# First stage of a hybrid SSD/MLP mixer: norm in 16 columns, tables and small loads moved, shift and scale between products, last three rows tile by tile

## The chip, the cores and the metric

The kernel runs on one core of a Trainium2 chip. Its engines work side by side, each with an instruction queue of its own: TensorE (PE, matrix products; the loading of its weights is listed apart as PEld), VectorE (DVE), ScalarE (ACT), GpSimd (POOL) and SyncE (SP), which here only issues loads. An instruction whose input is not ready holds up everything behind it on its engine. Large loads run on 16 DMA engines, in the order in which they are issued on a queue.

The metric is the device time of one execution in microseconds, as a median over several.

## What is computed by the reference

One layer (the depth is 1) of a mixer over 256 latent tokens with 256 context tokens as a prefix, all in float32, width 2048. Cut to what matters:

```python
shift, scale, gate = split(silu(c) @ w_ada + b_ada, 3)             # latent tokens
shift_c, scale_c, _ = split(silu(c_ctx) @ w_ada + b_ada, 3)        # context tokens
hc = rmsnorm(ctx, g_pre) * (1 + scale_c) + shift_c
hx = rmsnorm(x, g_pre) * (1 + scale) + shift
zc, zx = hc @ w_in[:, :XBC_W + DT_W], hx @ w_in
# both: depthwise convolution over tokens + SiLU, dt = softplus(z_dt + dt_bias)
y = bidirectional_ssd(...)          # latent scans start from the context's final states
y_a = rmsnorm((y + d_skip * xh) * silu(z_ssd), g_ssd)
y_b = rmsnorm(u * (w_s @ rmsnorm(v, g_v) + b_s) * silu(z_mlp), g_mlp)
x = x + gate * rmsnorm(concat(y_a, y_b) @ w_out, g_post)
```

The change lies in the first part: norm, shift, scale, h, and the first columns of z. What is computed behind it is as it was.

## The kernel before

**Layout.** Activations are held with channels on the 128 partitions and the 512 tokens (256 of context, then 256 latent) in columns. The 2048 channels are 16 blocks of 128, numbered by kt. A product in nearly full float32 precision is made of three: each operand is split into a rounded part (hi) and the rest (lo), and hi x hi, hi x lo and lo x hi are summed in PSUM (`mm3`, L124 to L126).

**The first stage** runs with PE, DVE and ACT in the order in which the program is written (`manual_schedule`). It has these steps.

- *Norm.* x arrives in four loads of four blocks (`xT`, L228). Each block is squared, even ones by ACT (L246), odd ones by DVE (L244); PE sums the squares over the partitions with a matrix of ones into `pss` (L248), one quarter of the partitions for each kt modulo 4. Warming products (L236) stand between. The sums are copied (L252), summed again and spread over all partitions by a product over 512 columns (L254), and Sqrt (L255) and reciprocal (L256) give the scale `rb`, 512 columns on all partitions.
- *Shift and scale.* `ada_mm` multiplies the conditioning vectors with one loaded tile of `w_ada` (1 MB; `ada`), as products with 32 columns of weights each into one of four quarters of the partitions (L209). There are 32 such tiles. They are grouped in units: a unit of one block kt takes two tiles (64 columns a product), a unit of two blocks takes four (128 columns). `ada_fin` ends a unit: DVE transposes the sums (L216), ACT adds biases and gains into `ha` and `hb` (L218, L220). Before, units 0 and 1 have one block, the others two.
- *h.* `make_h(kt)`: DVE multiplies x by scale and norm (L287), ACT adds the shift and rounds to hi (L290), DVE forms lo (L292).
- *Weights.* `wst` holds, for each kt, 64 columns for dt and seven tiles of 128 columns (`FIRST`). `split_st(kt)`: ACT rounds (L279), DVE forms the rests (L280 for dt, L281 for the tiles).
- *Products.* A row is one kt: psdt (two products of 512 columns, L360 and L361), then tiles 0 to 6 by three products each, tiles 3 and 6 over the latent 256 columns only. Each tile has its own PSUM sums over all 16 rows, so no tile is done before row 15. In rows 1 to 13 tiles of shift and scale for later rows, and in rows 1 to 14 `h` of the next, stand ahead of the row's products; in row 0 they stand between and behind them. In row 15 psdt and tiles 4 and 5 come first (`LAST`), then dt is brought to token order by PE (`dt_tok`, L300, L301) and put through a softplus on DVE and ACT (`dt_softplus`, L304 to L314), then come the other tiles.

**Loads** of this stage are issued by SP: x, the tiles of `w_ada` (six buffers) and `wst` (three). A load waits on SP until its buffer has been used. Three small ones (dt bias, A, D skip) are issued by POOL at the head, among constants that POOL builds.

**Behind it** come 25 more tiles of z (`wxbc`, split by L80 and L81), with convolution (L433, L446), SiLU and the SSD scans placed between their products by a list of due times (`later`, `pump`); there the scheduler orders the engines. A tile's PSUM is free again when its convolution has read it. Then follow the latent part (`wlat`) and the output projection.

## Time and profile before

| | |
|---|---|
| runs (median of 3) | 1017.2 us (1014.84 to 1017.51) |
| the profiled execution | 1015.47 us |
| its span, first to last instruction | 1013.7 us |
| mean granted clock of TensorE | 0.992 |
| first product row begins (L360) | 28.59 us |
| last pair of tiles of shift and scale begins (L209) | 120.45 us |
| first product of the next stage begins | 137.28 us |

Times in the profile's lines count from the first instruction. A line of the timeline gives start, duration, engine, line of the code, operation, output and inputs, how many instructions are merged, and in brackets how long the engine had been idle and what ended that. A matrix product's duration runs beyond the start of the next one, since products are pipelined: what a product costs in a stream is the distance of the starts. A line of the waits gives the wait in total, how often, and the longest.

### The profile page before, as it was taken

To read this page: it belongs to the slowest core of one execution; us is meant where nothing else is said; L and a number is where in the kernel's file an instruction comes from. 1 tells how busy PE (TensorE), PEld (TensorE's weight loads), DVE (VectorE), ACT (ScalarE), POOL (GpSimd) and SP (SyncE) were. 2 spreads that over 40 slices of the span, in tenths; PEclk is the share of its full clock that TensorE was granted. 3 is DMA by queue.
4 is the path that set the end of the run, shared out by engine and by line. 5 is a ranking of instruction groups with operands and counts; after the bars stand their busy time and mean duration, and the time that the engine had idled before them with its cause. 6 is when DMAs were issued, how large, how long until landed. Compare 5 with 4: busy or idle time off the path is not lost.

```text
span 1013.7 us, 14056 instructions
## 1 busy us (share of the span) xinstructions
PE 988.3 (97%) x5628; PEld 802.7 (79%) x5628; DVE 630.5 (62%) x954; ACT 469.1 (46%) x657; POOL 118.9 (12%) x161
## 2 busy tenths in 40 slices
PE   6899999989999999999999999999999999999996
PEld 2788887768887878787888888887888888888885
DVE  4544499886657575666567767666555564445626
ACT  3433357643534353444645433455565563346512
POOL 1000012652322322224000000000000000000000
PEclk9899999999999999999999999999999999999999
DMA  9999642122223222234787777774455545556622
GB/s 353 414 416 416 277 191 83 45 81 83 83 84 110 73 109 83 84 110 147 293 310 266 283 283 289 268 283 169 179 192 178 195 166 208 187 188 245 255 81 83
DMA packets 30033, 198.82 MB, mean 196 GB/s; under 512 B 3552, under 2 KB 3696, under 8 KB 7312
## 3 DMA queue, kind: packets, MB, share of 16 engines
q1 hardware_dynamic: 28224, 192.44, 50.5%
q0 software_dynamic: 1024, 4.28, 1.6%
q10 hardware_dynamic: 720, 1.20, 0.3%
q8 instruction: 44, 0.72, 0.3%
q14 instruction: 21, 0.17, 0.0%
HBM read 195.81 MB, written 2.10 MB: 195 GB/s over the span
## 4 chain that ended last, share of the span: by engine, by line
PE 77%; issue 9%; DVE 5%; DMA 5%; POOL 2%; ACT 1%; SPq 0%; DVEq 0%; POOLq 0%; ACTq 0%
PE psx L124 9%; PE psx L126 9%; PE psx L125 9%; PE pa L862 8%; PE pa L863 8%; PE pa L864 7%; PE pm L907 3%; PE pm L908 3%; PE pm L909 3%; PE psada L209 3%; PE pq L907 2%; PE pq L909 2%; PE pq L908 2%; DVE acc L446 2%; DMA ada<-in_wada_dram 2%
## 5 line engine op out<-in xcount | busy, mean ns | idle before, releaser
L81 DVE TENSOR_TENSOR lo_w<-w,hi_w 128x1024 fp32r<-128x1024 f32 x234 | 288.9, 1240 | 203.5 <-ACT hi_w L80 203.3
L80 ACT CAST hi_w<-w 128x1024 fp32r<-128x1024 f32 x234 | 245.8, 1052 | 314.2 <-PE pa L864 144.2
L862 PE MATMUL pa<-hi_w,hhi 128*128 128x512 f32 x512 | 201.9, 395 | 0.0
L863 PE MATMUL pa<-lo_w,hhi 128*128 128x512 f32 x512 | 199.8, 390 | 0.1
L864 PE MATMUL pa<-hi_w,hlo 128*128 128x512 f32 x512 | 199.4, 389 | 0.0
L124 PE MATMUL psx<-hhi,hi_w 128*128 128x512 f32 (+1 forms) x400 | 152.9, 382 | 2.4 <-DVE acc L446 2.4
L125 PE MATMUL psx<-hlo,hi_w 128*128 128x512 f32 (+1 forms) x400 | 146.3, 366 | 0.0
L126 PE MATMUL psx<-hhi,lo_w 128*128 128x512 f32 (+1 forms) x400 | 146.1, 365 | 0.0
L862 PEld LDWEIGHTS pa<-hi_w,hhi 128*128 128x128 f32 x512 | 96.2, 188 | 20.9 <-issue 1.6
L864 PEld LDWEIGHTS pa<-hi_w,hlo 128*128 128x128 f32 x512 | 96.1, 188 | 20.0
L863 PEld LDWEIGHTS pa<-lo_w,hhi 128*128 128x128 f32 x512 | 96.2, 188 | 19.9 <-DVE lo_w L81 0.5
L124 PEld LDWEIGHTS psx<-hhi,hi_w 128*128 128x128 f32 x400 | 75.6, 189 | 15.7 <-issue 5.0
L125 PEld LDWEIGHTS psx<-hlo,hi_w 128*128 128x128 f32 x400 | 75.6, 189 | 12.8 <-issue 1.9
L126 PEld LDWEIGHTS psx<-hhi,lo_w 128*128 128x128 f32 x400 | 75.5, 189 | 12.5 <-issue 0.2
L446 DVE SCALAR_TENSOR_TENSOR acc<-psx,pc,acc 128x248 f32<-128x248 f32 (+1 forms) x204 | 84.4, 468 | 1.4 <-ACT acc L433 0.7
L723 DVE SCALAR_TENSOR_TENSOR junk<-gate,cb 128x2048 bf16<-128x2048 f32 x16 | 36.6, 2289 | 22.2 <-DMA gate<-in_wada_dram 22.2
L907 PE MATMUL pm<-hi_w,hhi 128*128 128x512 f32 x128 | 50.0, 390 | 0.0
L908 PE MATMUL pm<-lo_w,hhi 128*128 128x512 f32 x128 | 49.9, 390 | 0.0
L909 PE MATMUL pm<-hi_w,hlo 128*128 128x512 f32 x128 | 49.7, 389 | 0.0
L124 PE MATMUL psx<-hhi,hi_st 128*128 128x512 f32 (+1 forms) x112 | 41.2, 368 | 0.0
L125 PE MATMUL psx<-hlo,hi_st 128*128 128x512 f32 (+1 forms) x112 | 40.6, 362 | 0.0
L126 PE MATMUL psx<-hhi,lo_st 128*128 128x512 f32 (+1 forms) x112 | 40.5, 362 | 0.0
(224 smaller groups left out, 1264.0 us busy)
## 6 DMA issues: line engine op xcount, KB each, us to landing
w<-in_wlat_dram SPq DMA_DIRECT2D x64, 1024.0 KB, 4.8
ada<-in_wada_dram SPq DMA_DIRECT2D x32, 1024.0 KB, 14.7
w<-in_wout_dram SPq DMA_DIRECT2D x32, 1024.0 KB, 4.8
w<-in_wxbc_dram SPq DMA_DIRECT2D x25, 1024.0 KB, 4.8
gate<-in_wada_dram SPq DMA_DIRECT2D x16, 1024.0 KB, 5.1
wst<-in_wst_dram SPq DMA_DIRECT2D x16, 480.0 KB, 14.1
xT<-in_xch_dram SPq DMA_DIRECT2D x4, 1024.0 KB, 10.1
xf<-in_xtok_dram SPq DMA_DIRECT2D x2, 1024.0 KB, 5.6
```

The source lines that it names most:

```text
L80: nc.scalar.copy(hi, raw)
L81: nc.vector.tensor_tensor(lo, raw, hi.bitcast(F32), op=ALU.subtract)
L124: nc.tensor.matmul(ps, lhsT=whi, rhs=hhi[k][:, s], start=start, stop=False)
L125: nc.tensor.matmul(ps, lhsT=whi, rhs=hlo[k][:, s], start=False, stop=False)
L126: nc.tensor.matmul(ps, lhsT=wlo, rhs=hhi[k][:, s], start=False, stop=stop)
L446: nc.vector.scalar_tensor_tensor(ao, zi, cw[:, k : k + 1], ao, op0=ALU.mult, op1=ALU.add)
L862: nc.tensor.matmul(pa[tk], lhsT=hhi[k][:, t], rhs=whi[:, w], start=k == 0, stop=False)
L863: nc.tensor.matmul(pa[tk], lhsT=hhi[k][:, t], rhs=wlo[:, w], start=False, stop=False)
L864: nc.tensor.matmul(pa[tk], lhsT=hlo[k][:, t], rhs=whi[:, w], start=False, stop=k == KT - 1)
L907: nc.tensor.matmul(p, lhsT=yh[:, t], rhs=whi[:, w], start=j == 0, stop=False)
L908: nc.tensor.matmul(p, lhsT=yh[:, t], rhs=wlo[:, w], start=False, stop=False)
L909: nc.tensor.matmul(p, lhsT=yl[:, t], rhs=whi[:, w], start=False, stop=hf == 0 and j == 15)
```

## The change

- *Head.* The three small loads move from POOL to SP, after the loads that row 4 issues. `sc` is cleared by DVE. Silu of the conditioning vectors and a first Sqrt come ahead of the squares on ACT. The first six tiles of `w_ada` and three `wst` blocks are issued ahead, `wst` 0 right after the first tile.
- *Norm.* The 512 sums are transposed in blocks of 32 (DVE), so that one product with a selecting matrix (`sel`) gives them in 16 columns; Sqrt and reciprocal work on 16 columns; a copy and a second block transpose spread the result over 512 columns again. Two more warming products stand behind the first two tiles of shift and scale.
- *Start.* Split 0 is made ahead of shift, scale and h of row 0.
- *Units.* Four units of one block, then six of two; the layout of `w_ada` in memory follows.
- *Between products.* `row_steps` puts each tile of shift and scale after the first, second or a later product tile of a row, no longer ahead of the row. In rows 0 to 2 `ada_fin`, `make_h` and `split_st` of the next row hang on the second of them; from row 3 on the splits stand at the row's beginning. Row 3 has four tiles, row 12 the last four, then h and split of rows 14 and 15.
- *Last rows.* Rows 13 to 15 run tile by tile: psdt, 4 and 5 of row 13; then psdt, tile 4, tile 5 in rows 14 and 15, dt's turn; then tiles 0, 1, 2, 3, 6 each over all three rows. Split 15 takes a buffer of the ring of `w_ada` tiles.

```diff
-    nc.gpsimd.dma_start(dtc, dtp[0:1].partition_broadcast(P))
...
-    nc.gpsimd.dma_start(dsk, dskip.partition_broadcast(P))
...
-    nc.gpsimd.dma_start(A, dtp[1:2].partition_broadcast(P))
...
     sc = stp.tile([P, KT, 32], F32, name="sc")
-    nc.gpsimd.memset(sc, 0.0)
+    nc.vector.memset(sc, 0.0)
...
-    nc.scalar.activation(sc[:, :, 0:2], sc2, AF.Silu)
-    tc.keep_in_program_order(nc.scalar.activation(sc2[:, 0, 0:1], epsc, AF.Sqrt))
+
+    sel = stp.tile([P, 4, 32], F32, name="sel")
+    nc.vector.tensor_reduce(sel[:, 0], ident.rearrange("p (g m) -> p m g", g=4), axis=mybir.AxisListType.X, op=ALU.add)
+    nc.vector.tensor_copy(sel[:, 1:4], bc(sel[:, 0], 1, 3))
...
-    UNITS = [(0,), (1,)] + [(m, m + 1) for m in range(2, KT, 2)]
+    UNITS = [(m,) for m in range(4)] + [(m, m + 1) for m in range(4, KT, 2)]
 
     def ada_place(ci):
 
-        if ci < 4:
+        if ci < 8:
             return ci // 2, 64, 8 * (ci % 2), 8
-        return ci // 4 + 1, 128, 4 * (ci % 4), 4
-
-    def ada_load(c0):
-        for ci in (c0, c0 + 1):
+        return ci // 4 + 2, 128, 4 * (ci % 4), 4
+
+    def ada_load(ci):
+        if ci < 2 * KT:
             ada_raw[ci] = load_raw(wada[ci], f"ada_{ci}")
...
+    wraw = {}
+
+    def wst_load(kt):
+        w = st3.tile([P, WST], F32, tag="wst", name=f"wst{kt}")
+        nc.sync.dma_start(w, wst[kt])
+        wraw[kt] = w
+
     for t in range(4):
         nc.sync.dma_start(xT[:, 4 * t : 4 * t + 4, :].rearrange("p k t -> p (k t)"), xch[t])
     ada_load(0)
+    wst_load(0)
+    ada_load(1)
+    ada_load(2)
+    ada_load(3)
+    wst_load(1)
+    ada_load(4)
+    ada_load(5)
+    wst_load(2)
+
+    nc.scalar.activation(sc[:, :, 0:2], sc2, AF.Silu)
+    nc.scalar.activation(sc2[:, 0, 0:1], epsc, AF.Sqrt)
 
 
     psw = spt([P, 512], "psw")
...
         nc.tensor.matmul(pss[32 * g : 32 * g + 32, :], lhsT=ones[:, 0:32], rhs=sq, start=k < 4, stop=k >= KT - 4)
         if g == 3:
             warm(1)
+
+
     rb, ss4 = yseg(4), yseg(5)
-    nc.vector.tensor_copy(ss4, pss)
-    psb = spt([P, TOK], "psb")
-    nc.tensor.matmul(psb, lhsT=ones, rhs=ss4, start=True, stop=True)
-    nc.scalar.activation(rb, psb, AF.Sqrt, bias=epsc, scale=1.0 / (32 * D))
-    nc.vector.reciprocal(rb, rb)
+    nc.vector.transpose(ss4, pss)
+    psb = spt([P, KT], "psb")
+    nc.tensor.matmul(psb, lhsT=sel.rearrange("p g m -> p (g m)"), rhs=ss4.rearrange("p (b i) -> p b i", i=32)[:, :, 0],
+                     start=True, stop=True)
+    rc = stp.tile([P, KT], F32, name="rc")
+    nc.scalar.activation(rc, psb, AF.Sqrt, bias=epsc, scale=1.0 / D)
+    nc.vector.reciprocal(rc, rc)
+    nc.vector.tensor_copy(ss4.rearrange("p (b i) -> p b i", i=32), bc(rc, 2, 32))
+    nc.vector.transpose(rb, ss4)
     ada_mm(0)
     ada_mm(1)
+    warm(2)
     psdt = spt([P, TOK], "psdt")
     psx = []
...
     def split_st(kt):
         raw = wraw[kt]
-        hi = wp["spl"].tile([P, WST + 64], F32R, tag="hi", name=f"hi_st{kt}")
-        lo = wp["spl"].tile([P, WST - 64], F32R, tag="lo", name=f"lo_st{kt}")
+        if kt < KT - 1:
+            hi = wp["spl"].tile([P, WST + 64], F32R, tag="hi", name=f"hi_st{kt}")
+            lo = wp["spl"].tile([P, WST - 64], F32R, tag="lo", name=f"lo_st{kt}")
+        else:
+            hl = wp["raw"].tile([P, 2048], F32R, tag="raw", name=f"hl_st{kt}")
+            hi, lo = hl[:, 0 : WST + 64], hl[:, WST + 64 : 2 * WST]
         nc.scalar.copy(hi[:, 64:], raw)
         nc.vector.tensor_tensor(hi[:, 0:64], raw[:, 0:64], hi[:, 64:P].bitcast(F32), op=ALU.subtract)
         nc.vector.tensor_tensor(lo, raw[:, 64:], hi[:, P:].bitcast(F32), op=ALU.subtract)
@@ -314,54 +335,80 @@
         nc.vector.scalar_tensor_tensor(pl, pl, 2.0, s1, op0=ALU.add, op1=ALU.mult)
 
     sp0 = {}
-    wst_load(0)
-    ada_load(2)
-    wst_load(1)
-    ada_load(4)
-    ada_fin(0)
-    make_h(0)
-    sp0[0] = split_st(0)
-    for kt in range(KT):
-        if kt + 2 < KT:
-            wst_load(kt + 2)
-        if kt + 3 < KT:
+
+    def prod(i, kt):
+        whi, wlo = sp0[kt]
+        if i < 0:
+            nc.tensor.matmul(psdt, lhsT=whi[:, 0:P], rhs=hhi[kt], start=kt == 0, stop=False)
+            nc.tensor.matmul(psdt, lhsT=whi[:, 0:P], rhs=hlo[kt], start=False, stop=kt == KT - 1)
+        else:
+            mm3(psx[i], whi[:, (i + 1) * P : (i + 2) * P], wlo[:, i * P : (i + 1) * P], kt,
+                kt == 0 and i < 6, kt == KT - 1 and i != 3, ORDER[FIRST[i]] >= 24)
+
+    ALL = [("m", i) for i in range(-1, NST)]
+
+    def row_steps(kt):
+
+
+        st_ = {n: [] for n in range(1, NST + 1)}
+        if kt < 3:
+            st_[2] = [("a", 2 * kt + 2)]
+            st_[3] = [("a", 2 * kt + 3), ("f", kt + 1), ("h", kt + 1), ("s", kt + 1)]
+        elif kt == 3:
+            st_[1] = [("s", 4)]
+            st_[2], st_[3], st_[4] = [("a", 8), ("a", 9)], [("a", 10)], [("a", 11), ("f", 4), ("h", 4)]
+        elif kt % 2 == 0:
+            st_[1] = [("h", kt + 1), ("s", kt + 1)]
+            st_[2], st_[3] = [("a", 2 * kt + 4)], [("a", 2 * kt + 5)]
+            if kt == FULL - 1:
+                st_[5] = [("a", 30)]
+                st_[6] = [("a", 31), ("f", 9), ("h", 14), ("s", 14), ("h", 15), ("s", 15)]
+        else:
+            st_[1] = [("s", kt + 1)]
+            st_[2], st_[3] = [("a", 2 * kt + 4)], [("a", 2 * kt + 5), ("f", kt // 2 + 3), ("h", kt + 1)]
+        out_ = [("m", -1, kt)]
+        for n in range(1, NST + 1):
+            out_ += st_[n] + [("m", n - 1, kt)]
+        return out_
+
+
+    FULL = KT - 3
+    steps = [("s", 0), ("f", 0), ("h", 0)]
+    for kt in range(FULL):
+        steps += [("l", kt)] + row_steps(kt)
+    steps += [("m", i, FULL) for i in LAST[:3]]
+    for n, i in enumerate(LAST):
+        steps += [("m", i, kt) for kt in range(FULL + (n < 3), KT)]
+        if i in (4, 5):
+            steps.append(("z", i - 4))
+        if n == 2:
+            steps.append(("t",))
+    for what, *ij in steps:
+        if what == "m":
+            prod(*ij)
+        elif what == "a":
+            ada_mm(*ij)
+        elif what == "f":
+            ada_fin(*ij)
+        elif what == "h":
+            make_h(*ij)
+        elif what == "s":
+            sp0[ij[0]] = split_st(*ij)
+        elif what == "l":
+            kt = ij[0]
             ada_load(2 * kt + 6)
-        whi, wlo = sp0[kt]
-        if kt + 1 < KT:
-            sp0[kt + 1] = split_st(kt + 1)
-        steps = [("m", -1)] + [("m", i) for i in range(NST)]
-        if kt == KT - 1:
-            steps = [("m", i) for i in LAST]
-            steps.insert(3, ("t", 0))
-            for i in range(2):
-                steps.insert(steps.index(("m", 4 + i)) + 1, ("z", i))
-        if kt == 0:
-            steps[1:1] = [("a", 2)]
-            steps[3:3] = [("a", 3)]
-            steps[5:5] = [("f", 1), ("h", 1)]
-            steps += [("a", 4), ("a", 5)]
-        elif kt + 1 < KT:
-            a = [("a", 2 * kt + 4), ("a", 2 * kt + 5)] if kt + 2 < KT else []
-            f = [("f", (kt + 1) // 2 + 1)] if kt % 2 else []
-            steps = a + f + [("h", kt + 1)] + steps
-        for what, i in steps:
-            if what == "a":
-                ada_mm(i)
-            elif what == "f":
-                ada_fin(i)
-            elif what == "h":
-                make_h(i)
-            elif what == "z":
-                nc.vector.tensor_copy((z4, z5)[i], psx[4 + i])
-            elif what == "t":
-                dt_tok()
-                dt_softplus()
-            elif i < 0:
-                nc.tensor.matmul(psdt, lhsT=whi[:, 0:P], rhs=hhi[kt], start=kt == 0, stop=False)
-                nc.tensor.matmul(psdt, lhsT=whi[:, 0:P], rhs=hlo[kt], start=False, stop=kt == KT - 1)
-            else:
-                mm3(psx[i], whi[:, (i + 1) * P : (i + 2) * P], wlo[:, i * P : (i + 1) * P], kt,
-                    kt == 0 and i < 6, kt == KT - 1 and i != 3, ORDER[FIRST[i]] >= 24)
+            ada_load(2 * kt + 7)
+            if kt + 3 < KT:
+                wst_load(kt + 3)
+            if kt == 4:
+                nc.sync.dma_start(dtc, dtp[0:1].partition_broadcast(P))
+                nc.sync.dma_start(A, dtp[1:2].partition_broadcast(P))
+                nc.sync.dma_start(dsk, dskip.partition_broadcast(P))
+        elif what == "z":
+            nc.vector.tensor_copy((z4, z5)[ij[0]], psx[4 + ij[0]])
+        elif what == "t":
+            dt_tok()
+            dt_softplus()
...
-    for kt in range(2):
+    for kt in range(4):
         wada[2 * kt : 2 * kt + 2] = ss[:, :, :, kt].reshape(2, 8, P, 256).transpose(0, 2, 1, 3).reshape(2, P, D)
-    for m in range(2, KT, 2):
+    for m in range(4, KT, 2):
```

More of the change, by code (lines that the diff above doesn't have):

```diff
@@ L265, in tile_hybrid_ssd_mlp @@
     psx[3] = psx[3][:, 0:256]
-    wraw = {}
-    def wst_load(kt):
-        w = st3.tile([P, WST], F32, tag="wst", name=f"wst{kt}")
-        nc.sync.dma_start(w, wst[kt])
-        wraw[kt] = w
     def split_st(kt):
         raw = wraw[kt]
-        hi = wp["spl"].tile([P, WST + 64], F32R, tag="hi", name=f"hi_st{kt}")
-        lo = wp["spl"].tile([P, WST - 64], F32R, tag="lo", name=f"lo_st{kt}")
+        if kt < KT - 1:
[4 more added lines that the diff above has]
+            hi, lo = hl[:, 0 : WST + 64], hl[:, WST + 64 : 2 * WST]
         nc.scalar.copy(hi[:, 64:], raw)
```

## The prediction

> **What bounds the kernel now.** The page first, then the time by stretches, then what TensorE (PE) waited for up to 240 us.
>
> ```profile
> span 1013.7 us, 14056 instructions
> PE 988.3 (97%) x5628; PEld 802.7 (79%) x5628; DVE 630.5 (62%) x954; ACT 469.1 (46%) x657; POOL 118.9 (12%) x161
> ```
>
> ```profile
> 40.00:60.00 20.00, 19.92 (x254) 16.39 (x248) 9.98 (x22) 7.50 (x17) 0.00 (x0) 1.00 1.02 416
> ...
> 140.00:160.00 20.00, 19.60 (x99) 16.00 (x98) 19.30 (x40) 10.70 (x14) 0.82 (x3) 1.00 0.16 54
> ...
> 200.00:220.00 20.00, 17.50 (x92) 13.77 (x91) 16.90 (x32) 9.62 (x14) 13.01 (x16) 1.00 0.29 105
> ```
>
> ```profile
> PE psdt L360 <- DVE hi_st L280: 5.4, 1, 5.4
> PE pss L248 <- ACT y L246: 4.6, 2, 3.7
> PE psx L124 <- DVE acc L446: 2.4, 1, 2.4
> ...
> PE psy L641 <- DVE M L624: 0.3, 1, 0.3
> PE psd L497 <- DVE y L480: 0.3, 1, 0.3
> ```
>
> The columns of a stretch are its length, then busy time of PE, weight load, DVE, ACT, POOL, then granted clock, DMA share, GB/s. PE is the bound almost everywhere. In the first stage the loads run at the full 416 GB/s too, yet PE never stands for them after 42 us. There is little to win: the 5.4 us before the first product row, the slow clock behind it, and 3.0 us (2.4 + 0.3 + 0.3) of waits for VectorE (DVE) after the stage, which DVE, full at 140 to 160 us, causes.
>
> **The start.** Before:
>
> ```profile
> 11.99 1.28 ACT L176 ACT_TABLE_LOAD   x1
> ...
> 13.53 1.28 ACT L177 ACT_TABLE_LOAD   x1
> ...
> 14.94 2.42 ACT L246 ACTIVATE y<-xT 128x512 f32<-128x512 f32 x4
> ...
> 19.37 0.69 DVE L252 COPY y<-pss 128x512 f32<-128x512 f32 x1 [1.40 <-PE pss L248]
> ...
> 21.17 1.99 PE L209 MATMUL psada<-ada,sc 128*32 128x64 f32 x128
> 21.28 0.69 ACT L255 ACTIVATE y<-psb,epsc 128x512 f32<-128x512 f32 x1 [3.92 <-PE psb L254]
> 22.00 3.35 DVE L256 RECIPROCAL y<-y 128x512 f32<-128x512 f32 x1 [1.94 <-ACT y L255]
> ...
> 25.27 0.19 DVE L216 STREAM_TRANSPOSE adat<-psada 128x64 f32<-128x64 f32 x1
> ...
> 26.49 0.91 ACT L290 ACTIVATE hhi<-xT,hb 128x256 fp32r<-128x256 f32 x2 [0.42 <-DVE xT L287]
> ...
> 28.59 0.80 PE L360 MATMUL psdt<-hhi,hi_st 128*128 128x512 f32 x1 [5.42 <-DVE hi_st L280]
> ```
>
> Both table loads and their two small activations stand between squares, so four squares run back to back after them. With the tables loaded while ACT waits for x anyway, the squares follow the loads of x:
>
> ```profile
> DMA to landing us min/median/max: 6.7/10.1/13.0
> ```
>
> The fourth load of x, issued at 2.7 us, lands by 15.7. Two squares by each engine (about 0.65 each) end at 17.1 and the last sum at 17.6, against 19.2: 1.5 earlier, so DVE can start at 17.85. The old way from the sums to the scale takes 19.37 to 25.35, 5.98. The new one: a 32-block transpose of 512 columns, a product with 16 columns, Sqrt and reciprocal of 16 columns, a copy of 512, a transpose of 512. No row has such a transpose. The 64- and 128-column ones (0.19 here, 0.32 below) give 2 ns a column and, as an estimate, 1.1 us for 512; bounds are 0.69 (the copy of the same shape) and 3.35 (the slowest row of that shape). I take 1.1, by slope. With 0.7 for the copy, 0.8 for the three small steps and five hand-overs of 0.1 that makes 4.2. The scale is ready at 22.05. The first split, now ahead, costs DVE 1.15; transpose to the end of hhi takes 25.27 to 27.40 = 2.13. First product at 25.4. The small loads that leave the head of the run are worth something too:
>
> ```profile
> q0 software_dynamic: 96, 0.08, 1.3%
> ```
>
> That is 1.3% of 140 us: 1.8 us of all engines. I take 1.0 of it (bounds 0 and 1.8). So 24.4 instead of 28.59: **-4.2** (bounds: +0.3 with both transposes at 3.35, -5.8 with 0.69 and 1.8). The second tile of shift and scale now queues behind the first split's weights. Its load has landed by 22.2 today (the second half of the row at 21.17); 0.49 MB ahead of it cost 1.2 at 416 GB/s, the 1.0 comes off, 1.0 of product and 2.2 of preparation follow: 25.6 at the latest, which I leave to the bounds.
>
> Then the clock:
>
> ```profile
> 22.00:24.00 2.00, 1.17 (x84) 1.00 (x72) 2.00 (x1) 0.00 (x0) 0.00 (x0) 1.00 1.02 426
> 24.00:26.00 2.00, 0.00 (x0) 0.00 (x0) 1.54 (x3) 0.51 (x2) 0.00 (x0) 0.92 1.00 410
> ...
> 30.00:32.00 2.00, 2.00 (x65) 1.83 (x58) 1.23 (x2) 0.09 (x1) 0.00 (x0) 0.50 0.99 413
> 32.00:34.00 2.00, 2.00 (x68) 1.45 (x67) 0.00 (x0) 0.00 (x0) 0.00 (x0) 0.88 1.07 428
> ```
>
> PE stopped at 23.2, the clock fell to half near 25.7 (0.92 is 1.68 us full, 0.32 half) and came back near 32.5. With two warming products and a first row at 24.4, PE stands too briefly for that. What this row lost comes from these:
>
> ```profile
> 41.54 0.50 PE L360 MATMUL psdt<-hhi,hi_st 128*128 128x512 f32 x1
> ```
>
> ```profile
> 113.72 1.96 PE L209 MATMUL psada<-ada,sc 128*32 128x128 f32 x64
> ...
> 120.45 1.95 PE L209 MATMUL psada<-ada,sc 128*32 128x128 f32 x64
> 122.33 0.50 PE L360 MATMUL psdt<-hhi,hi_st 128*128 128x512 f32 x1
> ...
> 127.09 0.39 PE L360 MATMUL psdt<-hhi,hi_st 128*128 128x512 f32 x1
> ...
> 131.75 0.39 PE L360 MATMUL psdt<-hhi,hi_st 128*128 128x512 f32 x1
> ...
> 137.28 0.40 PE L124 MATMUL psx<-hhi,hi_w 128*128 128x512 f32 x1
> ```
>
> A row of products takes 131.75 - 127.09 = 4.66: 0.47 for psdt, 0.70 for a full tile, 0.35 for a latent one. A pair of tiles of shift and scale takes 122.33 - 120.45 = 1.88, 0.94 each (a 64-column one 1.99/2 = 1.0). Row 0 lasted 28.59 to 41.54 = 12.95 and should have taken 4.66 + 2.0 + 3.76 + three switches: 11.0. **-1.95** (upper bound 0, if the clock is slow anyway).
>
> **Between products.** A row with one pair lasts 120.45 - 113.72 = 6.73; less 4.66 and 1.88 leaves 0.19 for switching to the 32-column products and back. Before, they stood in 15 places: two in row 0, the run over its end, one in each of rows 2 to 13. Now there are 29: two a row, three in row 3, four in row 12. 14 x 0.19 = **+2.7** (bounds 0, if the 0.19 belongs to the rows, and 3.5, at 0.25). Units 2 and 3 in 64 columns add 4 x 0.06 = **+0.2**.
>
> In rows 0 to 2 the next row's shift, scale, h and split now all hang on a tile placed after the third product. The chain behind such a tile:
>
> ```profile
> 122.47 0.32 DVE L216 STREAM_TRANSPOSE adat<-psada 128x128 f32<-128x128 f32 x1 [5.52 <-PE psada L209]
> 123.24 0.88 DVE L287 SCALAR_TENSOR_TENSOR xT<-xT,ha,y 128x256 f32<-128x256 f32 x2 [0.46 <-ACT ha L218]
> ...
> 125.66 0.23 DVE L280 TENSOR_TENSOR hi_st<-wst,hi_st 128x64 fp32r<-128x64 f32 x1 [0.41 <-ACT hi_st L279]
> 125.80 1.08 DVE L281 TENSOR_TENSOR lo_st<-wst,hi_st 128x896 fp32r<-128x896 f32 x1
> 126.80 0.87 DVE L287 SCALAR_TENSOR_TENSOR xT<-xT,ha,y 128x256 f32<-128x256 f32 x2
> ```
>
> From the tile's end (122.33) to the split's first part (125.89) are 3.56, for a single unit 3.5. PE has three full and two latent tiles left, 2.8, and 0.1 to switch: 0.6 short, three times, **+1.8** (bounds 0 and 2.9). From row 3 on the split goes ahead and the chain is about a us shorter: covered by those 2.9.
>
> **The last rows.** Row 12 carries four tiles. Behind the last stand transpose, h14, split14, h15, split15 on DVE and ACT, and the order on PE asks for psdt of rows 14 and 15 after only 3.0 us (two tiles, then three products of row 13, 2.92, and 0.1). Split14 comes at 3.56: 0.55 of waiting. Split15: h15 begins 126.80 - 122.33 = 4.47 behind, and h to split takes 125.89 - 123.24 = 2.65: 7.12, while PE is through with row 14's psdt at 4.0. Another 3.1. **+3.6** (bounds 2.6, and 4.9 if a split of the next weights, L81, slips in with its 1.2 to 1.3 a piece). Everything on PE queues behind these two products; nothing else there may pass them.
>
> The clock: the 2.4 us wait near 206 left it at 1.00, the idle time from 23.2 felled it after 2.5. Here 4.1 us pass with 0.47 of work; I take it that it falls. One slow stretch of 2 to 4 us at half speed costs 1 to 2: **+1.5** (bounds 0 and 1.95, what row 0 lost). [...]
>
> PE leaves the stage at 137.28 - 4.2 - 1.95 + 2.7 + 0.2 + 1.8 + 3.6 + 1.5 = 140.9: later by 3.6. In exchange psdt is complete some 13 us ahead of that (the twelve products of tiles 4 and 5 in rows 14 and 15 and all of the other five tiles are still to come, 12 us with dt's turn, and the slow clock), and DVE works on what it did late before:
>
> ```profile
> 135.45 0.41 DVE L301 TENSOR_TENSOR y<-pstok,dtc 128x256 f32<-128x256 f32 x1
> ...
> 150.43 0.41 DVE L480 SCALAR_TENSOR_TENSOR y<-dtt,y 128x256 f32<-128x256 f32 x1
> ```
>
> This chain ended 13 us behind PE's leaving. It starts when tiles 4 and 5 are through, at about 132.5, 8 us before PE leaves instead of 2, and the first convolutions follow tile by tile. That is 6 us and more of head start against waits of 3.0: **-3.0** (bounds 0 and -3.0; nothing else waits there).
>
> **At nothing.** Small loads in row 4: three issues on SP and 1.8 us of DMA; the loads move a row (2.59 MB at 416 GB/s) in 6.2 us against 6.9 for PE, six tiles ahead of use, and make that up in three rows. Without that lead the next tile of shift and scale is late by up to 1.8. The fifteenth row's split holds a load slot until the stage ends, so two later weight loads can queue on SP until 141; the first product that needs them is two tiles (22 us) off. The Silu and Sqrt ahead of the squares wait for a small load and end near 5, while ACT stood until 7.9 for x.
>
> **Sum:** +3.6 - 3.0 = +0.6. The profiled execution took 1015.47 (span 1013.7 and 1.8 around it) and becomes 1016.1; it lies 1.7 below the median of 1017.2, so on the median's scale **1017.8**, its own range 1015 to 1020.
>
> **Rivals**, on the same scale; about 0.3% (3.05 us) is what this kernel's measurement can tell from no change.
>
> 1. The clock holds in the last rows. For it: the clock that held over the 2.4 us near 206; against it: the fall near 25.7. 1017.8 - 1.5 = 1016.3. [...]
> 2. Slower: the waits after the stage stay. Place: the first product tiles after it, up to 206 us, where DVE is full. If DVE spends its head start waiting for PE's late dt products and for weights to split, instead of on dt and convolutions, the 3.0 stay: 1020.8. It decides if the dt addition (L301) starts less than 4.2 us ahead of PE's leaving the stage: the 1.8 of today and the 2.4 that are to be made up.
> 3. The switches cost nothing: 1017.8 - 2.7 = 1015.1. For it: one pair was only seen whole. Against: the products behind a pair take 127.09 - 122.33 = 4.76, the next row's, without one, 4.66.
> 4. The last rows do not wait: -3.6 - 1.5, 1012.7. It needs ACT and DVE to prepare two rows in 3 us; the rows above show 7.1.
> 5. The norm is not sooner, because the wide transposes cost like the reciprocal: 1017.8 + 4.2 = 1022.0.
>
> **Chances.** Forecast 0.36 (0.28 within 0.3%, 0.08 slower); clock holds 0.18 (0.15 within, 0.03 faster); waits stay 0.20 (0.15 slower, 0.05 within); switches free 0.14 (0.08 within, 0.06 faster); last rows do not wait 0.07 (faster); norm not sooner 0.05 (0.04 slower, 0.01 within). Together: faster 0.16, same 0.57, slower 0.27. The range reaches from just above rival 4 to rival 5: 1013.0 to 1022.0.
>
> **What would show it.** The first psdt product near 24.4 at a clock of 1.00; 0.6 us of PE waiting for L280's successor in each of rows 0 to 2; rows 4 to 11 at 6.9 us; a wait of about 3 us for the fifteenth split near 125 and a clock below 1.00 behind it; the first w product near 141; no wait for DVE acc near 206. The forecast is wrong if rows 4 to 11 keep 6.73, if psdt's fifteenth product comes without a wait, or if DVE is still behind at 200 us.

## The result, and the profile after

The changed kernel takes **1031.45 us** (1030.43 to 1032.23 in four runs) against 1016.6 for the kernel of before run beside it: 1.0148 times as long, 95% interval 1.0132 to 1.0163. The forecast was 1017.8 and no change; the time lies outside its range. The page, the waits of PE up to 240 us and the three stretches that were shown of before:

```profile
span 1028.7 us, 14324 instructions
PE 1000.1 (97%) x5760; PEld 805.0 (78%) x5760; DVE 627.9 (61%) x960; ACT 467.9 (45%) x656; POOL 119.6 (12%) x157
```

```profile
PE psd L544 <- DVE y L527: 5.0, 1, 5.0
PE psada L208 <- issue: 3.2, 2, 2.7
PE psdt L342 <- DVE hl_st L301: 2.8, 1, 2.8
...
PE psdt L342 <- DVE hi_st L301: 1.1, 3, 0.5
```

```profile
40.00:60.00 20.00, 16.79 (x295) 12.61 (x294) 5.11 (x12) 4.00 (x9) 0.00 (x0) 0.91 1.02 422
140.00:160.00 20.00, 15.02 (x69) 12.96 (x69) 18.44 (x37) 10.42 (x13) 3.07 (x3) 0.83 0.11 38
200.00:220.00 20.00, 20.00 (x114) 16.18 (x113) 13.96 (x30) 11.33 (x17) 13.21 (x17) 1.00 0.15 54
```

The wait of 5.4 ahead of the first row is gone, and so is that of 2.4 near 206. In their place PE stands in two stretches in which it was full: 3.2 of 20 us at 40 to 60, 5.0 at 140 to 160, with a clock of 0.91 and 0.83 there. The rows behind it, PE's own and in the second fence those of ACT and DVE after the last tile:

```profile
19.68 1.10 PE L208 MATMUL psada<-ada,sc 128*32 128x64 f32 x64 [1.39 <-DMA ada<-in_wada_dram]
...
23.09 0.50 PE L342 MATMUL psdt<-hhi,hi_st 128*128 128x512 f32 x1 [0.40 <-ACT hhi L311]
...
31.23 0.50 PE L342 MATMUL psdt<-hhi,hi_st 128*128 128x512 f32 x1 [0.48 <-DVE hi_st L301]
...
42.52 0.98 PE L208 MATMUL psada<-ada,sc 128*32 128x64 f32 x54
46.15 0.63 PE L208 MATMUL psada<-ada,sc 128*32 128x64 f32 x10 [2.65 <-issue]
...
56.56 0.38 PE L208 MATMUL psada<-ada,sc 128*32 128x128 f32 x2 [0.56 <-issue]
...
61.23 0.49 PE L342 MATMUL psdt<-hhi,hi_st 128*128 128x512 f32 x1
...
118.11 0.39 PE L342 MATMUL psdt<-hhi,hi_st 128*128 128x512 f32 x1
...
127.59 0.39 PE L342 MATMUL psdt<-hhi,hi_st 128*128 128x512 f32 x1
...
130.04 0.50 PE L342 MATMUL psdt<-hhi,hi_st 128*128 128x512 f32 x1 [0.43 <-DVE hi_st L301]
...
133.58 0.50 PE L342 MATMUL psdt<-hhi,hl_st 128*128 128x512 f32 x1 [2.80 <-DVE hl_st L301]
...
152.88 0.71 PE L544 MATMUL psd<-y,tri_lt 128*128 128x96 f32 x2 [4.98 <-DVE y L527]
...
155.00 0.77 PE L122 MATMUL psx<-hhi,hi_w 128*128 128x512 f32 x1
```

```profile
147.94 0.37 ACT L718 COPY y<-psx 128x256 f32<-128x256 f32 x1 [3.41 <-PE psx L124]
148.32 1.28 ACT L496 ACT_TABLE_LOAD   x1
149.62 0.63 ACT L496 ACTIVATE xbc<-acc 128x512 f32<-128x512 f32 x1
150.16 1.98 ACT L80 CAST hi_w<-w 128x1024 fp32r<-128x1024 f32 x2
```

```profile
139.52 0.42 DVE L322 TENSOR_TENSOR y<-pstok,dtc 128x256 f32<-128x256 f32 x1
...
152.32 0.41 DVE L527 SCALAR_TENSOR_TENSOR y<-dtt,y 128x256 f32<-128x256 f32 x1
152.66 1.63 DVE L493 SCALAR_TENSOR_TENSOR acc<-psx,pc,acc 128x252 f32<-128x252 f32 x4
154.21 2.34 DVE L81 TENSOR_TENSOR lo_w<-w,hi_w 128x1024 fp32r<-128x1024 f32 x2
```

The last tile ends at 147.9 (152.88 less 4.98). Two things stand between it and the first w product (a product with the next stage's weights, `hi_w` and `lo_w`). PE comes to the products that end dt (L544) first and waits 4.98 us for their input; they and that wait last until 155.0. In the trace of before the same products (L497) begin at 150.89, 13.6 us behind the first w product, and wait 0.28. And only at 150.16 does ACT begin to split the next weights, behind the copy of the last tile, a table load and a Silu. Of before, the row that answers to it stands during row 14, nine us ahead of the stage's end:

```profile
128.19 3.89 ACT L80 CAST hi_w<-w 128x1024 fp32r<-128x1024 f32 x4
```

With these rows the two spans can be set against each other, stretch by stretch:

| stretch | before | after | difference | forecast |
|---|---|---|---|---|
| start to the first psdt product | 28.59 | 23.09 | -5.5 | -4.2 |
| from there to psdt of row 13 | 93.74 | 104.50 | +10.8 | +2.75 |
| to the end of the last tile | 14.95 | 20.3 | +5.4 | +5.1 |
| to the first w product | 0 | 7.1 | +7.1 | 0 |
| to the end of the span | 876.4 | 873.7 | -2.7 | -3.0 |

The differences add up to 15.1, the spans differ by 15.0. Three rows came out near the forecast, the last of them by another cause (below); two did not, and the experiments are on these. In the runs with this start the first row came at 23.1 to 23.4, in three of them at 24.2 to 24.5; that much is the run's own.

### The profile page after: what moved, and what is told of

It reads as the page before. It is cut to its first block, busy times and chain, and to the rows that moved or that the text cites. A ratio compares the mean times of both kernels' runs of the same rounds, so it can differ in the third digit from the quotient of the medians.

```text
span 1028.7 us, 14324 instructions
## 1 busy us (share of the span) xinstructions
PE 1000.1 (97%) x5760; PEld 805.0 (78%) x5760; DVE 627.9 (61%) x960; ACT 467.9 (45%) x656; POOL 119.6 (12%) x157
## 4 chain that ended last, share of the span: by engine, by line
PE 92%; DVE 3%; ACT 2%; DMA 1%; POOL 1%; issue 1%; SPq 0%; DVEq 0%; ACTq 0%; POOLq 0%
PE pa L909 11%; PE pa L910 11%; PE pa L911 11%; PE psx L122 10%; PE psx L124 9%; PE psx L123 9%; PE psada L208 3%; PE pm L954 3%; PE pm L955 3%; PE pm L956 3%; PE pq L954 2%; PE pq L956 2%; PE pq L955 2%; DMA ada<-in_wada_dram 1%; PE pso L673 1%; PE psy L688 1%
## 5 line engine op out<-in xcount | busy, mean ns | idle before, releaser
L208 PE MATMUL psada<-ada,sc 128*32 128x128 f32 (+1 forms) x1280 | 35.4, 254 | 4.6 <-issue 3.2
L208 PEld LDWEIGHTS psada<-ada,sc 128*32 128x32 f32 x1280 | 27.4, 110 | 15.3 <-issue 12.9
## 6 DMA issues: line engine op xcount, KB each, us to landing
w<-in_wlat_dram SPq DMA_DIRECT2D x64, 1024.0 KB, 4.9
ada<-in_wada_dram SPq DMA_DIRECT2D x32, 1024.0 KB, 10.2
w<-in_wout_dram SPq DMA_DIRECT2D x32, 1024.0 KB, 4.8
w<-in_wxbc_dram SPq DMA_DIRECT2D x25, 1024.0 KB, 4.8
gate<-in_wada_dram SPq DMA_DIRECT2D x16, 1024.0 KB, 5.3
xT<-in_xch_dram SPq DMA_DIRECT2D x4, 1024.0 KB, 7.9
xf<-in_xtok_dram SPq DMA_DIRECT2D x2, 1024.0 KB, 5.6
```

Of the source, the lines that this page charges most:

```text
L208: nc.tensor.matmul(ps[32 * g : 32 * g + 32, 0:n], lhsT=sc[:, k, :], rhs=raw[:, o : o + n], start=k == 0, stop=k == KT - 1)
```

## Experiments

**What holds the next weights back.** Two theories for the 7.1 us: the order in which ACT and DVE were given their work, or the space of the split's buffers, which the fifteenth row's split shares. The first run forces the order:

```
+    split_to(2)
+    early = [getattr(x, "ins", x) for x in last]
     split_to(3)
+
+    def behind(fn, *a):
+        with tc.issue_after(early[0]), tc.issue_after(early[1]):
+            fn(*a)
...
-    nc.scalar.copy(z7, psx[6])
+    behind(nc.scalar.copy, z7, psx[6])
```

(the end of dt and the first two convolutions go through `behind` too; `last` holds the two instructions of the latest split.)

> The changed kernel with one order forced: the first two halves of the next weights (L80, L81) are split ahead of the first convolution, the copy of the last tile and the end of dt on ScalarE and VectorE; the rows are as they were. Changed kernel 1031.5 us. Theory A (the 7.3 us after the stage come from the order of ScalarE and VectorE, where the split stood behind the last tile's copy): the first w product follows the last tile within 1.5 us instead of 7.3, the clock holds there (1.7 more), so 1031.5 - 5.8 - 1.7 = 1024 us (1022 to 1026). Theory B (the space of the split's buffers comes free only with the last row's products): the split waits all the same, 1031.5 within 2. Theory C (the gain is given back, since the convolutions begin later and VectorE is late again near 200 us): up to 3.0 of it is lost, 1027.

1026.82 us, ratio 1.0099 (1.0084 to 1.0114). The rows of PE in the last rows, behind the stage, and later:

```profile
134.24 0.51 PE L343 MATMUL psdt<-hhi,hl_st 128*128 128x512 f32 x1 [2.81 <-DVE hl_st L302]
...
146.85 0.40 PE L123 MATMUL psx<-hhi,hi_w 128*128 128x512 f32 x1
147.08 0.40 PE L124 MATMUL psx<-hlo,hi_w 128*128 128x512 f32 x1
147.74 0.50 PE L125 MATMUL psx<-hhi,lo_w 128*128 128x512 f32 x1 [0.26 <-DVE lo_w L82]
...
217.61 0.47 PE L123 MATMUL psx<-hhi,hi_w 128*128 128x512 f32 x1 [1.97 <-DVE acc L494]
```

The first w product comes 8.15 us sooner, directly behind the last tile, with 0.26 of waiting and a product time of 0.40 instead of 0.77 (at a clock of 0.50 from 152 to 158 us in the changed kernel): theory A, as to the wait. Part of the 8.15 is another thing: behind the same wait of 2.8 in the last rows the products kept 0.39 in this execution (0.63 in the changed kernel), so that the rows took 1.7 us less. From the first w product to the end are 1024.0 - 146.85 = 877.1 instead of 873.7, and 2.0 us of it are a wait for DVE's convolutions again (L494, at 217.6): theory C, as to the total. The edit puts the split ahead and the end of dt behind it, both at once; how the 7.1 divides between the two is not shown. The other theory:

```
+            skip = wp["raw"].tile([P, 2048], F32R, tag="raw", name="skip")
+            nc.vector.memset(skip[:, 0:1].bitcast(F32), 0.0)
             hl = wp["raw"].tile([P, 2048], F32R, tag="raw", name=f"hl_st{kt}")
```

> The changed kernel with the fifteenth row's split in another load slot, whose place the first three split buffers of the next weights do not share; the orders of the engines stay. Theory A (order): no change, 1031.5 us within 2; the first w product stays some 7 us behind the last tile. Theory B (space): the split of the next weights no longer waits for the last row's products, 1031.5 - 7.3 - 1.7 = 1022.5.

1031.27 us, ratio 1.0148 (1.0130 to 1.0167), the same as the changed kernel: the space that the fifteenth split takes is not it. Then the last three rows as a whole, row by row again:

```
-    FULL = KT - 3
+    FULL = KT - 1
...
-    steps += [("m", i, FULL) for i in LAST[:3]]
     for n, i in enumerate(LAST):
-        steps += [("m", i, kt) for kt in range(FULL + (n < 3), KT)]
+        steps += [("m", i, FULL)]
```

(with tiles 30 and 31 in row 13 and the fifteenth split in its own buffer)

> The changed kernel with its last three rows row by row again (tile by tile only in row 15, shift and scale of tiles 30 and 31 in row 13, the fifteenth split in its own buffer); start and insertions stay. Theory A (the tile-by-tile order costs 5.2 in the rows and 7.3 + 1.7 behind them, and brings 2.7 later): 1031.5 - 14.2 + 2.7 = 1020 us (1017 to 1022), and rows 0 to 12 still 10 us longer than before. Rival (the loss is made in rows 0 to 12 and only surfaces behind the stage): 1028 or more.

1019.01 us, ratio 1.0026 (1.0015 to 1.0038). So 12.4 of the 14.8 us that were lost hang on the tile-by-tile order: its own waits and slow clock, and the orders of the engines behind it. Without it the first w product stands at 142.98, directly behind the last tile.

**What takes the start back.** The other loss, +10.8 in rows 0 to 12, remains in that run: from the first row to psdt of row 14, ahead of which both kernels have all tiles of shift and scale, it is +9.8. The start by itself, on the kernel of before:

```
-    nc.vector.tensor_copy(ss4, pss)
+    nc.vector.transpose(ss4, pss)
...
+    sp0[0] = split_st(0)
     ada_fin(0)
     make_h(0)
-    sp0[0] = split_st(0)
     for kt in range(KT):
```

(the whole new norm, the early tables, the late small loads and the order of the first loads; units, rows and last rows are those of before)

> The kernel of before with the new start alone (norm by 16 columns, tables early, small loads in row 4, first split ahead); shift and scale stay at the head of the rows, the last rows row by row. Before: 1016.6 us. Theory A (the start is won and nothing takes it back): first product row at 23.1 instead of 28.6 and no slow clock in row 0, 1016.6 - 5.5 - 1.95 = 1009 us (1008 to 1012). Theory B (the first rows are short of loads or of instructions behind full DMA queues as soon as PE starts sooner): PE waits 2 to 5 us in the rows up to 60 us and it ends at 1012 to 1016.

1015.74 us, ratio 0.9994 (0.9984 to 1.0003): theory B. The first row is at 23.11, and then:

```profile
30.71 2.29 PE L208 MATMUL psada<-ada,sc 128*32 128x128 f32 x64
35.50 1.93 PE L208 MATMUL psada<-ada,sc 128*32 128x128 f32 x32 [2.50 <-DMA ada<-in_wada_dram]
38.05 1.94 PE L208 MATMUL psada<-ada,sc 128*32 128x128 f32 x32 [0.62 <-DMA ada<-in_wada_dram]
39.92 0.80 PE L374 MATMUL psdt<-hhi,hi_st 128*128 128x512 f32 x1
```

Tiles 6 and 7 are asked for at 33 and land at 35.4 and 38.0; the clock falls meanwhile (0.50 at 36 to 40 us, 0.75 at 40 to 44, a psdt product of 0.80). In the kernel of before PE came late enough not to wait for these loads (its waits up to 240 us name none). The changed kernel gets past these loads with units of 64 columns, which need two tiles a row instead of four. It pays in another coin: the two waits inside a tile that the profile puts down to "issue", time in which the engine waited for nothing that the profile shows. Inside a tile a product needs nothing that the tile's first product did not need. Three runs are on these waits and one on the price of the insertions. First, eight instructions fewer ahead of the wait (the run has 5756 products instead of 5760, and as many weight loads):

```
     ada_mm(1)
-    warm(2)
```

> The changed kernel without the two warming products behind the second tile of shift and scale: four product pieces and four weight loads, 8 instructions, fewer on TensorE ahead of the row-2 wait of 2.65 us that no semaphore explains. Theory I (TensorE runs out of instructions at the border of a block of 256): the same wait comes 8 instructions later in the work, behind piece 58 of the 64 of that tile instead of piece 54, about as long. Theory II (the wait belongs to the tile, its load, or a point in time): still behind piece 54, or at 43.5 us wherever that falls. The time is not what is asked; the clock may fall in row 0 and cost up to 2 us.

```profile
44.24 1.08 PE L208 MATMUL psada<-ada,sc 128*32 128x64 f32 x58
47.88 0.31 PE L208 MATMUL psada<-ada,sc 128*32 128x64 f32 x6 [2.56 <-issue]
```

Behind piece 58, as theory I has it (one run, 1032.0 us; a piece is one product of a tile). Then fewer loads queued ahead:

```
-    wp["raw"] = st.enter_context(mkpool(name="raw0", bufs=6, side="right"))
+    wp["raw"] = st.enter_context(mkpool(name="raw0", bufs=4, side="right"))
```

> The changed kernel with four load slots for the tiles of shift and scale instead of six, so that fewer loads are queued ahead. Theory I with the loads as its cause (the block of instructions stands behind loads already queued): the median from issue to landing of those tiles falls from 14.3 us to about 10 and the wait inside a tile near 44 us falls below 1.5 us; TensorE may wait for loads instead, which is a wait at the head of a tile and named as one. Rival (a block takes its 7 us whatever is queued): still 2.65. Time 1028 to 1035.

```profile
45.69 0.41 PE L208 MATMUL psada<-ada,sc 128*32 128x64 f32 x10 [2.12 <-issue]
```

```profile
ada<-in_wada_dram SPq DMA_DIRECT2D x19, 1024.0 KB, 10.2
```

1029.0 us, one run. The loads' median from issue to landing, up to 70 us, falls from 14.3 to 10.2 as expected, the wait only from 2.65 to 2.12: nearer to the rival. The clock holds here (1.00 at 46 to 50, against 0.54 and 0.61). Then the same tiles asked for faster, side by side in rows 0 to 3 and with four slots too, in the kernel with the rows of before from row 4 (below):

```
-            st_[2] = [("a", 2 * kt + 2)]
-            st_[3] = [("a", 2 * kt + 3), ("f", kt + 1), ("h", kt + 1), ("s", kt + 1)]
+            st_[2] = [("a", 2 * kt + 2), ("a", 2 * kt + 3), ("f", kt + 1), ("h", kt + 1), ("s", kt + 1)]
```

> The run with the rows of before from row 4 on (1017.8 us), with four load slots and with the tiles of shift and scale of rows 0 to 3 side by side behind the first product tile: three switches and the waits for the next row's split are gone there, so TensorE asks for the same instructions in less time. Theory I (a block of 256 instructions takes about 7 us to come while the loads run): what the rows win, the waits inside tiles take back; waits that no semaphore explains add up to more than 3 us and row 3 begins at 49 us or later (49.5 with four slots alone). If instructions are no limit: rows of 7.0 us, row 3 at 44.5 to 46.

```profile
37.89 0.28 PE L123 MATMUL psx<-hlo,hi_st 128*128 128x256 f32 x1 [0.43 <-issue]
38.12 0.39 PE L338 MATMUL psdt<-hhi,hi_st 128*128 128x512 f32 x1
39.37 1.92 PE L208 MATMUL psada<-ada,sc 128*32 128x64 f32 x121
44.47 0.32 PE L208 MATMUL psada<-ada,sc 128*32 128x64 f32 x7 [3.19 <-issue]
...
49.86 0.39 PE L338 MATMUL psdt<-hhi,hi_st 128*128 128x512 f32 x1
```

1018.06 us in one run. Theory I: row 3 at 49.86 in spite of shorter rows (some of it is the slow clock behind the wait, 0.70 at 44 to 48 us). And the places can be counted. From the product at 37.89 to piece 121 there are 2 products of the last tile, 2 of psdt, 3 of the first tile and 121, together 128, each with its weight load: 256 instructions. The changed kernel has such a small gap too, 0.3 ahead of the second row here (the other products of this size follow each other in 0.12):

```profile
38.16 0.28 PE L122 MATMUL psx<-hhi,hi_st 128*128 128x256 f32 x1
38.58 0.28 PE L123 MATMUL psx<-hlo,hi_st 128*128 128x256 f32 x1
```

From 38.58 to piece 54 there are again 2 + 2 + 3 + 64 + 3 + 54 = 128. To the third gap, the 0.56 at 56.56, 127 are recorded.

The traces have one more thing on this. The profile's DMA view has a queue of kind instruction, q8, whose packets by their number are PE's (last section). In the changed kernel one begins at 36.2, one at 43.8 and one at 54.2 us, each lasting 0.9 to 1.0, and PE goes on at 38.58, 46.15 and 56.56: 2.3 to 2.4 behind the start of a packet, three times. Together with the wait that moved by four pieces when four products were left out ahead of it, this speaks for the instructions as what PE stands for.

Last, the price of the insertions:

```
-            st_[2], st_[3] = [("a", 2 * kt + 4)], [("a", 2 * kt + 5)]
+            st_[3] = [("a", 2 * kt + 4), ("a", 2 * kt + 5)]
```

(and the same in the odd rows)

> The changed kernel with the two tiles of shift and scale of rows 4 to 12 side by side behind the second product tile instead of one product tile apart: one insertion a row instead of two. If an insertion costs what the rows say (7.11 - 4.66 - 1.88 = 0.57 for two), rows 4 to 11 fall to 6.8 us and the kernel to 1031.5 - 9 x 0.28 = 1029. If the 0.57 belongs to something else in the row (waits for splits, the load of the chip), they stay at 7.1.

```profile
102.32 0.39 PE L342 MATMUL psdt<-hhi,hi_st 128*128 128x512 f32 x1
109.06 0.39 PE L342 MATMUL psdt<-hhi,hi_st 128*128 128x512 f32 x1
```

6.74 a row, against 7.06 for such a row in the changed kernel (the mean over its rows 4 to 11 is (118.11 - 61.23) / 8 = 7.11): a second insertion in a row costs 0.3, a first one the 0.2 that it cost at the row's head. 1027.5 us, one run, in which the products also kept 0.39 behind the last rows' wait of 2.80.

**Put together.** First the new start with rows 0 to 3 of the changed kernel and the rows of before from row 4:

```
     def row_steps(kt):
+        if kt >= 4:
+            a = [("a", 2 * kt + 4), ("a", 2 * kt + 5)] if kt < KT - 2 else []
+            f = [("f", kt // 2 + 3)] if kt % 2 else []
+            return [("s", kt + 1)] + a + f + [("h", kt + 1)] + [("m", i, kt) for i in range(-1, NST)]
```

> The new start with 64-column units and insertions in rows 0 to 3, from row 4 on the rows of before: a pair at the head of each row, the last rows row by row. Against the run with row-by-row last rows (1019.0 us) only the insertions of rows 4 to 13 are gone. Theory A (each costs 0.19 more than a switch at the row's head, two a row): 1019.0 - 10 x 0.38 = 1015.2 us (1013.5 to 1017). Rival (what the rows win, the waits behind the stage take back): 1018 or more. Rows 0 to 3 should still lose in the wait inside a tile what the start has won, so that row 4 begins near 61 us as in all versions.

1017.77 us, ratio 1.0006 (0.9995 to 1.0017): between the two, nearer to the rival. The first w product moves from 142.98 to 138.92 as theory A has it, and 2.6 of these 4.1 are given back behind it, where the wait of 2.39 for DVE is there again and, this time, the clock falls behind it (0.91 at 210 to 225 us):

```profile
209.40 0.76 PE L122 MATMUL psx<-hhi,hi_w 128*128 128x512 f32 x1 [2.39 <-DVE acc L489]
```

Then the remedy that the run with the start alone suggests: leave the units of before and ask for tiles 6 and 7 later in row 1. The edit also moves the other tiles of shift and scale off the heads of their rows.

```
         if kt == 0:
-            steps[1:1] = [("a", 2)]
-            steps[3:3] = [("a", 3)]
-            steps[5:5] = [("f", 1), ("h", 1)]
-            steps += [("a", 4), ("a", 5)]
+            steps[2:2] = [("a", 2), ("a", 3), ("f", 1), ("h", 1)]
+        elif kt == 1:
+            steps[6:6] = [("a", 6), ("a", 7), ("f", 2), ("h", 2)]
+            steps[3:3] = [("a", 4), ("a", 5)]
         elif kt + 1 < KT:
...
-            steps = a + f + [("h", kt + 1)] + steps
+            steps[3:3] = a + f + [("h", kt + 1)]
```

> The new start on the kernel of before, with the tiles of shift and scale moved back inside their row: in row 0 behind the first product tile, in row 1 two behind the second and two behind the fifth, from row 2 on both behind the second; units of one and two tiles as before, one switch a row more at most; last rows row by row. In the run with the start alone TensorE waited 2.5 and 0.6 us for the loads of tiles 6 and 7 at the head of row 1 (landed 35.4 and 38.0) and lost the clock. Theory A (only the place of these two tiles hands the start back): row 2 begins at 41 to 43 us instead of 47.6, row 4 at 55 to 57 instead of 61.1, no wait inside a tile, and the kernel takes 1015.7 - 5 = 1011 us (1009 to 1013). Rival (the loads are the bound up to 60 us whatever the order): TensorE waits for later tiles instead, row 4 at 59 or later, 1014 to 1016. Rival (the waits behind the stage take it back): row 4 at 55 to 57 and 1013 to 1016 all the same.

**1009.31 us**, ratio **0.9925** (0.9910 to 0.9940): 7.6 us faster than before, the fastest of all versions.

```profile
37.73 1.96 PE L208 MATMUL psada<-ada,sc 128*32 128x128 f32 x64
42.06 0.50 PE L374 MATMUL psdt<-hhi,hi_st 128*128 128x512 f32 x1 [1.13 <-ACT hhi L304]
...
55.92 0.40 PE L374 MATMUL psdt<-hhi,hi_st 128*128 128x512 f32 x1
```

No wait for a load behind the first row, none inside a tile, a clock of 1.00 from 20 to 64 us, row 2 and row 4 where theory A had them. The same places with the old start:

> The kernel of before with its old start, and the tiles of shift and scale inside their rows as in the run that took 1009.3 us. Theory A (the start is what is won, the place of the tiles only lets it through): with the old start the loads are there in time anyway, so the place alone is worth little: first row still near 28.6, row 4 at 60 to 62 us, 1016.9 within 2. Rival (the place of the tiles by itself wins, by saving switches or waits): 1012 or less.

1015.77 us, ratio 0.9989 (0.9979 to 0.9998): theory A. Start alone 0.9994, place alone 0.9989, both 0.9925. The first w product stands at 136.75, 139.51 and 133.46, against 137.28 before. With the new place the start brings 6.0 us up to there, with the old one 0.5: the start is what wins, and the place of the tiles decides whether it arrives. Whether tiles 6 and 7 alone would do was not tried. The profiled executions of before and of both together differ by 6.1 us: 3.8 of these lie ahead of the first w product, 2.3 behind it, where the wait near 206 is missing (see the last table).

## Why the prediction was wrong

**The start** (-4.2, measured -5.5) was right in its mechanism as to the norm. DVE began on the sums at 16.09 instead of 17.85, the two transposes took 0.72 and 0.71 instead of 1.1, and the scale was ready at 19.13 instead of 22.05. Of these 2.9 us only 1.3 reached the first row, since the second tile of shift and scale, which the prediction left to its bounds, then came last: PE waited 1.39 for its load, until 19.68. What the small loads that left the head brought (1.0 said) was not tried apart. The slow clock of row 0 (-1.95) went as said (1.00 at 20 to 46 us); a new one of about the same size came in row 2 (1.6 us, from 0.54 at 46.15 to 48 and 0.61 at 48 to 50).

**Between products** is the first step that failed, twice. Its 0.19 came from one pair in a row, "switching to the 32-column products and back", and was multiplied by 14. With products, tiles, waits and slow clock taken out of each row, the 29 insertions cost 9.4 us in the trace of after (0.57 a row in rows 4 to 11, 1.06 in row 12, 3.8 in rows 0 to 3), the 15 of before 2.85: +6.5, not +2.7. The upper bound given, 3.5, was too low as well, since it priced each at no more than 0.25. And the prediction put at nothing the waits for PE's instructions, of which the new units of 64 columns need twice as many a tile (64 products instead of 32): +3.5 in three waits. Against that, the next row's split cost 0.7 instead of +1.8. With the clock and the +0.2 for the units that makes 10.6 of the 10.8.

**The last rows** were right: 0.43 and 2.80 of waiting (0.55 and 3.1 forecast), a clock that falls behind them (0.73 at 134 to 136, 0.50 at 136 to 138), +5.4 instead of +5.1. Rival 1, the clock holds, did not come true in this execution. The fall is partly luck, though: behind the same wait the products kept 0.39 in two of the runs above (split ahead, and pairs side by side), against 0.63 here.

**"In exchange"** and **"At nothing"** are where the largest term was missed. The head start was there as worked out: the dt addition (now L322) began at 139.52, 8.4 us ahead of the last tile's end, where 8 were said. But the chain still ended at 152.7, because DVE was given a convolution step between most of its steps, and PE was given the dt products ahead of the first w product: that is the wait of 4.98. And "two later weight loads can queue ... the first product that needs them is two tiles (22 us) off" looked at the later loads and passed over the first: its split had stood in row 14 by ACT's order, under cover of the rows, and came behind them in the new form of these rows. Split from 150.16 on, its first half could not have been ready before about 151.2 (two casts took 1.98), 3.3 us behind the last tile. So the step that failed is that the engines' orders behind the stage were taken to stay as they were, at nothing: +7.1. The run with the order forced shows that the orders cost it, the run with the space moved speaks against the other cause. How the 7.1 divides, and why the orders were built so, is not shown.

**The -3.0** came out (-2.7), but by luck, not by its reason. If the head start of dt were the cause, runs without it would keep the wait near 206, and the run with it would not have it. First w product, the rest of the span from there, and that wait:

| kernel | first w product | rest | wait |
|---|---|---|---|
| before | 137.28 | 876.4 | 2.4 |
| start only | 136.75 | 878.1 | 2.4 |
| rows of before | 138.92 | 876.8 | 2.4 |
| split ahead (head start) | 146.85 | 877.1 | 2.0 |
| after (head start) | 155.00 | 873.7 | none |
| by row | 142.98 | 874.2 | none |
| pairs late | 133.46 | 874.1 | none |
| place only | 139.51 | 874.6 | none |

The wait comes and goes with each new order of the engines' work, with and without a head start. Which difference of the orders decides is open.

None of the three signs of being wrong that the prediction named came up: rows 4 to 11 were longer, the fifteenth split was waited for, and DVE was not behind at 200 us. What it also named, the first w product near 141, is what would have told: it came at 155.0. The rivals: none held the outcome. "Slower" was given 0.27, on the waits after the stage; the trace went slower through work that the forecast had taken as covered.

## What to carry to other kernels

An engine that is never seen waiting for loads may only be late enough not to: before a start is made sooner, compare when each later tile lands with when it will then be asked for, and move its place along (here no gain that stands clear of the noise against 0.75%). When the order of a stage is written anew, look up where the next stage's first work stands in the orders of all engines; it is part of the change although no line of it was edited. Price an insertion by the row that has as many of them as the new one will, not by a row that has one.

## What the hardware showed

**PE's instructions.** The queue that is taken for that of PE's instructions, from the page of after:

```profile
q8 instruction: 45, 0.74, 0.3%
```

These are 45 packets of 16.4 KB, and PE had 5760 products and 5760 weight loads: 256 for each packet. Before, there were 44 for 5628 of each, in the run of both together 44 for 5632. This agreement is why the queue is taken for PE's. At a DMA share of 1.01 to 1.04 (38 to 46 us) PE used up 256 instructions in 4.9 us (38.58 to 43.5; 3.4 with the tiles side by side) and then stood, for 2.65 us (3.19 with the tiles side by side). From the end of one gap to the end of the next are 7.6 us, then 10.4, and 6.6 with the tiles side by side; what sets this time is not shown. Whether a packet would come sooner beside idle DMA engines was not tried: in rows 4 to 11 PE needs some 10 us for 256 instructions (87 products and as many weight loads in 7.1 us), and its waits name no such gap there.

**The clock.** In these rows the length of a stand does not by itself tell whether the clock falls. It fell behind stands of 2.65 us (after, in row 2, 0.54 at 46 to 48), 2.56 (without the warming products, 0.68 at 48 to 50 and 0.50 at 50 to 52), 2.80 (after, in the last rows, 0.73 at 134 to 136), 2.39 near 209 (rows of before, 0.91 at 210 to 225) and even 1.97 (split ahead, 0.89 at 210 to 225, with a product of 0.63 at 218.30). It held behind 2.12 (four slots, 1.00 at 46 to 50) and behind the 2.39 near 206 of before (1.00 at 206 to 212), and the products kept 0.39 behind 2.81 and 2.80 in the last rows (split ahead, pairs side by side). So 1.97 was enough in one place, and 2.81 was not in another; what decides is not shown.
